# Modulations moved to VectorE, memory keys moved into the norms, and the last product in token order, in a fused two-block model

## The chip, the cores and the metric

The kernel runs as one launch on one core of a Trainium2 chip. The metric is the device time of one launch in microseconds (us). The engines of the core work side by side, each with its own queue of instructions in a fixed order: TensorE (PE) multiplies matrices, VectorE (DVE), ScalarE (ACT) and GpSimd (POOL) compute element by element, SyncE (SP) issues the DMA transfers. An instruction starts when it is at the head of its queue and the semaphores that it waits for have been raised.

## The reference

Two blocks are computed one after the other for 256 tokens of width 1024, each with two layers, all in float32.

```python
for l in range(2):                                   # block 1
    mod = silu(c) @ w_ada[l] + b_ada[l]              # 1024 x 6144
    sh1, sc1, g1, sh2, sc2, g2 = split(mod, 6)
    h = rmsnorm(x, norm_mix_g[l]) * (1 + sc1) + sh1
    o = four_attention_mixers(h @ w_in[l])
    x = x + g1 * (o @ w_out[l])
    h = rmsnorm(x, norm_mlp_g[l]) * (1 + sc2) + sh2
    x = x + g2 * (square(relu(h @ w_up[l])) @ w_down[l])
x = rmsnorm(x, final_norm_g)
for l in range(2):                                   # block 2
    proj = x @ w_in_2[l]
    mem_kv = mem @ w_mem_kv_2[l]                     # keys and values of 256 memory tokens
    merged = gates . (ssd(proj), diff_attention(proj), cross_attention(proj, mem_kv))
    x = layernorm(sqrt(2) * x + merged @ w_out_2[l])
```

## The kernel before, in words

All weights come as pieces of 128x1024 floats (512 KB). `stream` lists the pieces in the order in which they are wanted, and `next_w` hands out the next one. When it does so, it also issues the DMAs of the first 8 pieces of the list and splits the first 4 of them. A piece is loaded by SyncE into one of 8 buffers `w` (L290), cast by ScalarE to a rounded high half `wh` (L300), and VectorE subtracts this from it for a low half `wl` (L302). There are 4 buffers of each half. The `w` buffer is free after the subtraction; the halves are free when PE has used them. PE multiplies by both halves: `gemm` makes 24 matmuls of a piece, in the order wh x high, wh x low, wl x high part of the activations, and all of its matmuls carry the line of `mm` (L328).

The pieces of `w_ada` are not split. A modulation (one of six column blocks of `mod`, for each of two layers) has 8 pieces, used in four steps of two. Nine of the twelve are multiplied on PE by `ada_step` (64 narrow matmuls into a bank called ada); three are computed on GpSimd by `ada_pool` in the MLPs, as a scaled sum of the pieces row by row (`rows`), of which `ada_rows` then sums the 128 partitions by four matmuls with ones. `ada_end` transposes the result and adds the bias.

Work that PE can do while something else is computed stands in a queue `e.q`, as closures under a tag: `add` appends, `fill(n)` emits the next n, `need(tag)` emits all up to the last one of a tag. So the order in which the program is written decides what stands between two steps of a chain. On each engine a scheduler may bring instructions marked by `high_priority` forward; `issue_after(i)` keeps an instruction behind instruction i.

The MLP of block 1 runs over 16 groups g: w_up of group g (two pieces into a bank g), then w_down of group g-1 (two pieces into four banks acc). The eviction of bank g is relu and square on ScalarE (L1005, L1008) and two operations on VectorE (L1009, L1010). The norms of block 1 are `rms_wide`: squares on ScalarE, folds on VectorE, a sum over partitions on PE (`st`), variance on VectorE (`rv`), the power -1/2 on GpSimd (`rsy`), a broadcast on PE (`bc`), and then `norm_apply` or, in the last norm, a split into xh and xl. In block 2 the first products of a layer are written to banks dt and g. The memory's keys (4 groups of two pieces) and values (2 groups of four) of layer 0 are computed at the start and in the last norm of block 1, those of layer 1 in the layernorm between the layers of block 2 (`mem_gemm`).

Of the kernel before, what the change touches and what calls it, by code (L numbers as in the profile page):

```python
# [16 lines left out]
P = 128  # L17
# [198 lines left out]
NW, NS = 8, 4  # L216
AHEAD_W, AHEAD_S = 8, 4
SPLIT_FIRST, NORM_FIRST = 100, 200
NU = 11
# [6 lines left out]
class Emit:  # L226
# [64 lines left out]

    def _split(self, ent):
        nc = self.nc
        key, _, w, _ = ent
        if key[0].startswith(("w_ada", "cmp_")):
            ent[3] = w
            return
# [29 lines left out]
    def mm(self, o, l, r, start, stop):  # L327
        self.nc.tensor.matmul(o, l, r, start=start, stop=stop)  # L328
# [37 lines left out]
    def tok_mm(self, ps, t, act, k, w, j, st, sp):  # L366

        wh, wl = (x[:, j * 512 : (j + 1) * 512] for x in w)
# [116 lines left out]
def block1(e, ctx, mem0):  # L485
# [3 lines left out]
    mhl, mk0, mv0 = mem0  # L489
# [13 lines left out]
    mlp_keys = lambda l: {1 + 6 * i + n: [("w_ada", *p, n)] for i, p in enumerate(ad_mlp(l)) for n in range(4)}  # L503
    MEM = 5
    a0 = ada(0, 0) + ada(0, 1)
    start = [[], a0[0:2], a0[2:4], a0[4:6], a0[6:8]]
    for k in range(MEM):
        e.stream(MEM_KEYS(0)[k], *start[k])
    for l in range(DEPTH):
# [11 lines left out]
        e.stream(("w_down", l, 15), *([("w_in1", l + 1, zorder[0])] if l + 1 < DEPTH else []), *ad_next(l))  # L521
    e.stream(*MEM_KEYS(0)[MEM:])

# [12 lines left out]
    boxes = {}  # L536
# [24 lines left out]
    def ada_pool(l, s, n):  # L561
# [1146 lines left out]
```

## Time and profile before

| | us |
|---|---|
| runs | 1838.72, 1840.98, 1836.07 |
| median | 1838.72 |
| profiled execution | 1837.75 |
| its span, first to last instruction | 1835.9 |
| PE busy in the span | 1785.1 (97%) |
| VectorE busy | 1332.7 (73%) |
| ScalarE busy | 1017.0 (55%) |
| GpSimd busy | 360.6 (20%) |

The mean granted clock of PE in the span is 0.990. The busy times of different engines lie beside each other, so they don't add up to the span.

### The profile page before, as it was taken

How to read it: one execution, taken by the hardware profiler on the slowest of the kernel's cores; microseconds unless marked ns; L12 is line 12 of the kernel's file. 1: busy time of each engine (PE TensorE's matmuls, PEld its weight loads, DVE VectorE, ACT ScalarE, POOL GpSimd, SP SyncE). 2: the span in 40 equal slices, each digit the busy share in tenths (PEclk: the TensorE clock that was granted, in tenths of full speed). 3: DMA queues.
4: the chain of work that ended last, by engine and by line, in shares of the span. 5: the costliest groups of instructions: out<-in, count | busy, mean ns of one | idle time of the engine just before them, and what ended most of it. 6: DMA issues, size and time to landing. Idle time of an engine off the chain costs nothing.

```text
span 1835.9 us, 36208 instructions
## 1 busy us (share of the span) xinstructions
PE 1785.1 (97%) x14320; PEld 1671.4 (91%) x14320; DVE 1332.7 (73%) x2204; ACT 1017.0 (55%) x1882; POOL 360.6 (20%) x291
## 2 busy tenths in 40 slices
PE   7999899999998999999999999999999999999997
PEld 6778799987878999998999999999998999999996
DVE  3566775756768655798897997566788797997565
ACT  4444444444554444567777575454556777575452
POOL 0000282800007300002444202200001444202200
PEclk9999999999998999999999999999999999999999
DMA  8874876768347655553444644465554445644451
GB/s 330 305 233 159 316 259 199 254 201 294 128 143 280 225 181 184 170 170 122 159 162 152 195 159 145 167 206 174 196 175 138 150 154 158 194 162 162 151 183 57
DMA packets 98219, 346.82 MB, mean 189 GB/s; under 512 B 12288, under 2 KB 13440, under 8 KB 97792
## 3 DMA queue, kind: packets, MB, share of 16 engines
q1 hardware_dynamic: 98048, 344.50, 55.7%
q8 instruction: 112, 1.84, 0.4%
q14 instruction: 59, 0.48, 0.1%
HBM read 339.01 MB, written 1.05 MB: 185 GB/s over the span
## 4 chain that ended last, share of the span: by engine, by line
PE 91%; DVE 3%; ACT 3%; DMA 2%; issue 1%; POOL 0%; SPq 0%; POOLq 0%; DVEq 0%; ACTq 0%
PE g L328 68%; PE acc L328 10%; PE yps L328 2%; PE ada L328 1%; PE o L328 1%; DVE wl L302 1%; PE sc L328 1%; PE ds L328 1%; ACT wh L300 1%; PE do L328 1%; PE xs L328 1%; PE xo L328 1%; ACT sb L666 1%; DMA w<-w_up 1%; PE tp L691 1%
## 5 line engine op out<-in xcount | busy, mean ns | idle before, releaser
L302 DVE TENSOR_TENSOR wl<-w,wh 128x1024 fp32r<-128x1024 f32 x518 | 664.5, 1286 | 345.5 <-ACT wh L300 342.4
L300 ACT CAST wh<-w 128x1024 fp32r<-128x1024 f32 x518 | 540.7, 1047 | 504.6 <-PE g L328 339.5
L328 PE MATMUL g<-xh,wh 128*128 128x256 f32 x1664 | 477.7, 287 | 2.1 <-ACT dv L1291 1.9
L328 PE MATMUL g<-xl,wh 128*128 128x256 f32 x1664 | 472.1, 284 | 0.0
L328 PE MATMUL g<-xh,wl 128*128 128x256 f32 x1664 | 471.5, 283 | 0.0
L328 PEld LDWEIGHTS g<-xh,wh 128*128 128x128 f32 x1664 | 319.2, 192 | 14.5 <-issue 6.2
L328 PEld LDWEIGHTS g<-xl,wh 128*128 128x128 f32 x1664 | 319.5, 192 | 0.9 <-issue 0.7
L328 PEld LDWEIGHTS g<-xh,wl 128*128 128x128 f32 x1664 | 319.6, 192 | 0.0
L328 PE MATMUL g<-ah,wh 128*128 128x256 f32 x736 | 212.1, 290 | 6.8 <-ACT ah L591 6.7
L328 PE MATMUL g<-ah,wl 128*128 128x256 f32 x736 | 211.6, 288 | 1.2 <-DVE wl L302 1.2
L328 PE MATMUL g<-al,wh 128*128 128x256 f32 x736 | 211.5, 288 | 0.7 <-DVE al L592 0.5
L394 POOL TENSOR_TENSOR rsy<-rv,mhalf 128x2 f32<-128x2 f32 (+1 forms) x14 | 15.2, 1088 | 937.6 <-DVE rv L411 828.4
L328 PE MATMUL acc<-pt,wh 128*128 128x256 f32 x1024 | 182.9, 280 | 0.0
L1485 POOL PARTITION_BROADCAST E<-rows x64 | 95.2, 1547 | 387.9 <-PE tw L1192 185.4
L328 PEld LDWEIGHTS acc<-pt,wh 128*128 128x128 f32 x1024 | 156.8, 188 | 0.5 <-issue 0.4
L1484 ACT ACTIVATE E<-E,ltok 128x128 f32<-128x128 f32 x384 | 124.4, 394 | 59.2 <-POOL E L1485 55.5
L328 PEld LDWEIGHTS g<-ah,wh 128*128 128x128 f32 x736 | 143.0, 195 | 11.0 <-ACT ah L591 7.6
L328 PEld LDWEIGHTS g<-al,wh 128*128 128x128 f32 x736 | 143.5, 195 | 2.8 <-DVE al L592 2.0
L328 PEld LDWEIGHTS g<-ah,wl 128*128 128x128 f32 x736 | 143.4, 195 | 2.3 <-DVE wl L302 1.6
L328 PE MATMUL acc<-pt,wl 128*128 128x256 f32 x512 | 142.3, 279 | 0.0
L570 POOL TENSOR_SCALAR sb<-w,ca 128x1024 f32<-128x1024 f32 x24 | 90.0, 3750 | 61.9 <-PE ada L328 32.8
L328 PEld LDWEIGHTS acc<-pt,wl 128*128 128x128 f32 x512 | 96.2, 188 | 0.0
(384 smaller groups left out, 3386.3 us busy)
## 6 DMA issues: line engine op xcount, KB each, us to landing
w<-w_ada SPq DMA_DIRECT2D x96, 512.0 KB
w<-w_up SPq DMA_DIRECT2D x64, 512.0 KB
w<-w_down SPq DMA_DIRECT2D x64, 512.0 KB
w<-w_br SPq DMA_DIRECT2D x64, 512.0 KB
w<-w_gl SPq DMA_DIRECT2D x48, 512.0 KB
w<-w_in SPq DMA_DIRECT2D x36, 512.0 KB
w<-w_xs SPq DMA_DIRECT2D x32, 512.0 KB
w<-w_z SPq DMA_DIRECT2D x32, 512.0 KB
```

Of the source, the lines that this page charges most:

```text
L300: nc.scalar.copy(wh, w)
L302: nc.vector.tensor_tensor(wl, w, wh.bitcast(F32), ALU.subtract)
L328: self.nc.tensor.matmul(o, l, r, start=start, stop=stop)
L394: self.nc.gpsimd.tensor_tensor(y, v, self.mhalf[:, 0:cols], ALU.pow)
L570: nc.gpsimd.tensor_scalar(dst, w, ca[:, 2 * n + i : 2 * n + i + 1], None, ALU.mult)
L666: nc.scalar.activation(self.src(i), self.src(i), AF.Exp, bias=nmx[:, i : i + 1], scale=scale, accum_out=den[:, i : i + 1])
L691: nc.tensor.transpose(tp[:, h * P : (h + 1) * P], src(h), e.ident)
L1484: ex = lambda o, s, r: nc.scalar.activation(o, o, AF.Exp, bias=bias[:, s, r : r + 1])
L1485: nc.gpsimd.partition_broadcast(E, state["rows"][32 * (h % 4) : 32 * (h % 4) + 1, :])
```

## The change

- `ada_vec` takes the place of `ada_pool`: the scaled sum of a modulation's pieces runs on VectorE, one multiply-add of 128x1024 for each piece. `issue_after(last["ev"].ins)` puts each behind the latest eviction of an MLP bank. Six modulations go this way, five of them in layer 0's MLP and one in layer 1's; PE keeps six.
- `next_w` splits up to 4 pieces that need it and loads up to 6 others ahead, unsplit ones or `w_ada`; the `w` buffers go from 8 to 6.
- The keys of layer 1's memory are computed in block 1, in the norms (`filler`, `mem_fill`); `rms_wide` emits a given number of fillers before the statistics, between them and the broadcast, and behind it. Only the values stay in block 2's layernorm. Layer 0's last value group fills the last norm as before.
- At the start, half of a memory group stands behind the last modulation.
- The last product finishes the first 128 tokens, then the others in two halves of 256 columns.

```diff
-NW, NS = 8, 4
-AHEAD_W, AHEAD_S = 8, 4
+NW, NS = 6, 4
...
     def next_w(self, *key):
-        for i, ent in enumerate(self.wq[:AHEAD_W]):
-            self._fetch(ent)
-            if i < AHEAD_S and ent[3] is None:
-                self._split(ent)
+        split = raw = 0
+        for ent in self.wq:
+            if not self._whole(ent) and split < NS:
+                split += 1
+                self._fetch(ent)
+                if ent[3] is None:
+                    self._split(ent)
+            elif raw < NW:
+                raw += 1
+                self._fetch(ent)
+                if self._whole(ent):
+                    ent[3] = ent[2]
+            else:
+                break
...
-    def rms_wide(self, pool, x, eps):
+    def rms_wide(self, pool, x, eps, before=0, between=0, behind=0):
         box = []
+        self.fill(before)
         with self.tc.high_priority(offset=NORM_FIRST):
             for j in range(4):
                 self.square(pool, box, flat(x[:, 2 * j : 2 * j + 2, :]))
-            return self.rstd(pool, self.fold_sum(box), D, eps)
+            st = self.fold_sum(box)
+        with self.tc.issue_after(self.last_mm.ins):
+            self.fill(between)
+        with self.tc.high_priority(offset=NORM_FIRST):
+            bc = self.rstd(pool, st, D, eps)
+        with self.tc.issue_after(self.last_mm.ins):
+            self.fill(behind)
+        return bc
...
-    ad_early = lambda l: ada(l, 2) if l == 0 else []
+    ad_early = lambda l: ada(0, 2) if l == 0 else ada(1, 4)
-    ad_norm = lambda l: ada(l,5) if l == 0 else ada(l,4)
-    ad_mlp = lambda l: [(1,0),(1,1)] if l == 0 else [(1,5)]
-    ad_next = lambda l: ada(l+1,2)+ada(l+1,3)
+    ad_mlp = lambda l: [k for p in ([(0, 5)] + [(1, s) for s in range(4)] if l == 0 else [(1, 5)]) for k in ada(*p)]
+    def mlp_keys(l):
+        out = {}
+        for j, key in enumerate(ad_mlp(l)):
+            out.setdefault(1 + (3 * j // 4 if l == 0 else 2 * j), []).append(key)
+        return out
+    mem1 = MEM_KEYS(1)
+    filler = [mem1[0:1], mem1[3:4], mem1[1:3], MEM_KEYS(0)[MEM:]]
...
-        e.stream(("w_out1", l, 2), ("w_out1", l, 3), ("w_up", l, 0), *ad_norm(l))
+        e.stream(("w_out1", l, 2), ("w_out1", l, 3), ("w_up", l, 0), *filler[l], ("w_up", l, 1))
         nxt = mlp_keys(l)
         for g in range(16):
+            e.stream(*nxt.get(g, []))
+            if g > 1:
+                e.stream(("w_up", l, g))
             if g >= 1:
-                e.stream(("w_up", l, g))
                 e.stream(("w_down", l, g - 1))
-            e.stream(*nxt.get(g, []))
...
-    def ada_pool(l, s, n):
+    def ada_vec(l, s, n):
         if n == 0:
-            boxes[l, s] = e.t(ap_, [P, 1536], "sb", bufs=2)[:, 0:D]
+            i = boxes["n"] = boxes.get("n", -1) + 1
+            if i % 2 == 0:
+                boxes["rows"] = e.unit("rows")
+            boxes[l, s] = boxes["rows"][:, i % 2 * D : (i % 2 + 1) * D]
         rows = boxes[l, s]
         for i in range(2):
-            nc.gpsimd.tensor_scalar(dst, w, ca[:, 2 * n + i : 2 * n + i + 1], None, ALU.mult)
-            if not first:
-                nc.gpsimd.tensor_tensor(rows, rows, dst, ALU.add)
+            w, c = e.next_w("w_ada", l, s, n), ca[:, 2 * n + i : 2 * n + i + 1]
+            with tc.issue_after(last["ev"].ins):
+                if n == 0 and i == 0:
+                    nc.vector.tensor_scalar(rows, w, c, None, ALU.mult)
+                else:
+                    nc.vector.scalar_tensor_tensor(rows, w, c, rows, ALU.mult, ALU.add)
+        if n == 3:
+            e.q.insert(min(6, len(e.q)), ("mlp", lambda: ada_rows(l, s)))
...
         if l:
-            bc0 = norm_stats(x)
+            bc0 = norm_stats(x, 2, 1, 1)
             e.need("next")
...
-        ada_add("norm", ad_norm(l))
-        bc0 = norm_stats(x)
+        mem_fill("norm", filler[l])
+        bc0 = norm_stats(x, 1, 1)
...
-        ada_add("next", ad_next(l))
+        mem_fill("next", filler[DEPTH + l])
...
-        for t in range(2):
-            ps = e.gbank("g")
-            for k in range(KC):
-                e.tok_mm(ps, t, hl, k, ws[k // 2], k % 2, k == 0, k == KC - 1)
-            ev(ps, 1, t)
-            norm(t)
+        for t, cols in ((0, (0, 512)), (1, (0, S)), (1, (S, 512))):
+            ps = e.gbank("g")[:, cols[0] : cols[1]]
+            with tc.issue_after(e.last_mm.ins):
+                for k in range(KC):
+                    e.tok_mm(ps, t, hl, k, ws[k // 2], k % 2, k == 0, k == KC - 1, cols)
+            ev(ps, 512 + cols[0], t)
+            if cols[1] == 512:
+                norm(t)
...
-        for i in range(6):
+        for i in range(4, 6):
             mem_gemm(e, l + 1, i, mhl, nmk, nmv)
```

How the instructions lie now is seen at three places. The first is VectorE's queue in layer 0's MLP before the change: L302 makes a low half wl of a piece w, L1009 and L1010 evict a bank g of w_up.

```order
L302 TENSOR_TENSOR wl_2569<-w_2471,wh_2567 128x1024
L302 TENSOR_TENSOR wl_2579<-w_2503,wh_2577 128x1024
L302 TENSOR_TENSOR wl_2667<-w_2571,wh_2665 128x1024
L302 TENSOR_TENSOR wl_2697<-w_2581,wh_2695 128x1024
L1009 TENSOR_TENSOR pt_461_2633<-pt_461_2633,g_2576 128x512
L1010 TENSOR_TENSOR pt_462_2635<-pt_461_2633,pt_462_2635 128x512
L302 TENSOR_TENSOR wl_2706<-w_2607,wh_2704 128x1024
```

An eviction stands behind four splits. After the change VectorE's queue in the same MLP reads as follows; L1054 and L1055 are the eviction, L604 is the new multiply-add on a piece of `w_ada` (w_2596, w_2599), L301 the split. w_2765 and w_2801 are the two w_up pieces of group 4, w_2831 and w_2861 those of w_down in group 3, g_2738 the bank of w_up in group 3.

```order
L1054 TENSOR_TENSOR pt_483_2795<-pt_483_2795,g_2738 128x512
L1055 TENSOR_TENSOR pt_484_2797<-pt_483_2795,pt_484_2797 128x512
L604 SCALAR_TENSOR_TENSOR rows_2588<-w_2596,ca_99,rows_2588 128x1024
L604 SCALAR_TENSOR_TENSOR rows_2588<-w_2599,ca_99,rows_2588 128x1024
L301 TENSOR_TENSOR wl_2769<-w_2765,wh_2767 128x1024
L301 TENSOR_TENSOR wl_2805<-w_2801,wh_2803 128x1024
L301 TENSOR_TENSOR wl_2835<-w_2831,wh_2833 128x1024
L301 TENSOR_TENSOR wl_2865<-w_2861,wh_2863 128x1024
L1054 TENSOR_TENSOR pt_500_2928<-pt_500_2928,g_2871 128x512
L1055 TENSOR_TENSOR pt_501_2930<-pt_500_2928,pt_501_2930 128x512
```

Two modulation pieces now stand between the eviction of group 3's bank and the splits for group 4. The DMAs of these pieces in SyncE's queue after the change:

```order
L289 DMA w_2596<-w_ada 128x1024
L289 DMA w_2599<-w_ada 128x1024
L289 DMA w_2602<-w_up 128x1024
L289 DMA w_2606<-w_up 128x1024
L289 DMA w_2636<-w_down 128x1024
L289 DMA w_2672<-w_down 128x1024
L289 DMA w_2702<-w_ada 128x1024
L289 DMA w_2732<-w_ada 128x1024
L289 DMA w_2735<-w_ada 128x1024
L289 DMA w_2739<-w_ada 128x1024
L289 DMA w_2765<-w_up 128x1024
L289 DMA w_2801<-w_up 128x1024
```

The load of w_2765 stands behind those of four further modulation pieces. In the built program it waits for VectorE's L604 on w_2596, whose buffer it takes, and the load of w_2801 for that on w_2599; the load of w_2702 waits for the multiply-add ahead of these.

The third place is PE's queue in the layernorm between the layers of block 2, where st is the sum for the variance, bc the broadcast, and g_ banks with mh and ml are memory products. Before the change the broadcast stands among memory products:

```order
L328 MATMUL g_15232<-wl_15090,mh_14644 128x512
L328 MATMUL g_15232<-wh_15088,ml_14645 128x512
L328 MATMUL g_15239<-wh_15088,mh_14644 128x512
L328 MATMUL bc_15127<-pack_1_70,rsy_15125 128x128 x2
L328 MATMUL g_15239<-wl_15090,mh_14644 128x512
```

After the change the last memory product, the statistics, the broadcast and the first product of the next layer (dt, from xh) follow one another:

```order
L337 MATMUL g_15181<-wl_15170,mh_14803 128x512
L337 MATMUL g_15181<-wh_15168,ml_14804 128x512
L337 MATMUL st_15207<-ones_72,fold_15120 128x1 x2
L337 MATMUL bc_15214<-pack_1_70,rsy_15212 128x128 x2
L337 MATMUL dt_15293<-xh_15255,wh_15188 128x256
L337 MATMUL g_15332<-xh_15255,wh_15217 128x256
L337 MATMUL g_15394<-xh_15255,wh_15294 128x256
L337 MATMUL dt_15293<-xl_15256,wh_15188 128x256
L337 MATMUL dt_15293<-xh_15255,wl_15190 128x256
```

The memory products that stood behind the broadcast are gone from here.

## Rows read from the trace of the kernel before

**Rows 1.** The page's part 1, share of the span of each engine.

```profile
PE 1785.1 (97%) x14320; PEld 1671.4 (91%) x14320; DVE 1332.7 (73%) x2204; ACT 1017.0 (55%) x1882; POOL 360.6 (20%) x291
```

**Rows 2.** Windows: the MLP of layer 0 (window, length, busy us (instructions) by engine, granted clock, DMA).

```profile
232.00:396.00 164.00, 164.00 (x1386) 162.91 (x1385) 108.19 (x89) 76.23 (x87) 82.60 (x26) 1.00 0.69 228
```

**Rows 3.** Chain of waits in two groups of that MLP (start, length, what).

```profile
268.87 5.76 PE g L328 x48
274.63 5.66 PE acc L328 x48
```

**Rows 4.** Timeline of DVE in the same groups (start, length, operation, idle before and its releaser).

```profile
272.75 1.23 DVE L302 TENSOR_TENSOR wl<-w,wh 128x1024 fp32r<-128x1024 f32 x1 [1.65 <-ACT wh L300]
...
276.79 0.69 DVE L1009 TENSOR_TENSOR pt<-pt,g 128x512 f32<-128x512 f32 x1
277.52 0.69 DVE L1010 TENSOR_TENSOR pt<-pt,pt 128x512 fp32r<-128x512 f32 x1
```

**Rows 5.** Timeline of ACT in the same groups.

```profile
271.67 1.05 ACT L300 CAST wh<-w 128x1024 fp32r<-128x1024 f32 x1 [1.83 <-PE g L328]
...
275.50 0.59 ACT L1005 ACTIVATE pt<-g 128x512 f32<-128x512 f32 x1
```

**Rows 6.** Timeline of SyncE's DMA issues, before the MLP and within it.

```profile
205.43 1.87 SPq L290 DMA_DIRECT2D w<-w_up  x2
...
258.01 0.80 SPq L290 DMA_DIRECT2D w<-w_up  x2
```

**Rows 7.** Timeline of PE where it waits (start, norm and last norm of block 1, attention).

```profile
62.31 0.50 PE L328 MATMUL g<-ah,wh 128*128 128x256 f32 x2 [2.53 <-ACT ah L591]
...
204.72 3.66 PE L328 MATMUL ada<-w,ca 128*32 128x256 f32 x64
...
210.02 0.71 PE L328 MATMUL bc<-pack,rsy 128*128 128x128 f32 x4 [1.10 <-POOL rsy L394]
...
408.18 0.64 PE L328 MATMUL ada<-w,ca 128*32 128x256 f32 x8 [1.36 <-DMA w<-w_ada]
...
481.68 1.08 PE L328 MATMUL o<-pt,z 128*64 128x256 f32 x4 [2.13 <-ACT pt L693]
...
554.00 1.22 PE L328 MATMUL bc<-pack,rsy 128*128 128x128 f32 x4 [4.49 <-POOL rsy L394]
...
757.53 0.71 PE L328 MATMUL bc<-pack,rsy 128*128 128x128 f32 x4 [1.05 <-POOL rsy L394]
...
759.36 0.38 PE L328 MATMUL dt<-xh,wh 128*128 128x256 f32 x1 [1.12 <-ACT xh L455]
```

**Rows 8.** Windows behind four of these waits (PEclk is the granted clock).

```profile
213.70:220.50 6.80, 6.21 (x27) 5.92 (x28) 6.24 (x15) 3.13 (x8) 3.36 (x2) 0.50 1.03 418
...
481.00:484.50 3.50, 2.82 (x23) 1.92 (x24) 3.42 (x16) 1.37 (x4) 0.00 (x0) 1.00 0.05 19
...
551.60:561.80 10.20, 6.29 (x28) 6.18 (x29) 7.06 (x16) 2.91 (x7) 7.22 (x3) 0.50 1.01 408
...
759.80:763.20 3.40, 3.40 (x18) 3.38 (x17) 3.40 (x10) 1.72 (x5) 0.00 (x0) 0.50 0.43 147
```

**Rows 9.** Groups by form: DVE's multiply-add of 128x1024 (count, busy us, mean ns).

```profile
L1221 DVE SCALAR_TENSOR_TENSOR r<-r,mv,gb 128x1024 f32<-128x1024 f32 x2 | 2.6, 1276 | 0.0
```

**Rows 10.** Timeline of ACT ahead of that MLP.

```profile
209.14 1.04 ACT L300 CAST wh<-w 128x1024 fp32r<-128x1024 f32 x1 [2.71 <-DMA w<-w_up]
```

**Rows 11.** Timeline of DVE in the second block's layernorm.

```profile
1292.19 0.16 DVE L411 TENSOR_SCALAR rv<-st 128x2 f32<-128x2 f32 x1 [1.39 <-PE st L328]
...
1296.92 0.86 DVE L1671 SCALAR_TENSOR_TENSOR lt<-r,pack,bc 128x256 f32<-128x256 f32 x2
```

**Rows 12.** Timeline of GpSimd (POOL) there.

```profile
1292.44 0.73 POOL L394 TENSOR_TENSOR rsy<-rv,mhalf 128x2 f32<-128x2 f32 x1 [126.06 <-DVE rv L411]
```

**Rows 13.** Chain of waits at the end of the span.

```profile
1825.83 0.69 DVE r L1212
...
1829.85 0.17 DVE rv L1219
...
1831.63 0.75 DVE r L1224
```

More of the change, by code (lines that the diff above doesn't have):

```diff
@@ L327, in mm @@
     def mm(self, o, l, r, start, stop):
-        self.nc.tensor.matmul(o, l, r, start=start, stop=stop)
+        self.last_mm = self.nc.tensor.matmul(o, l, r, start=start, stop=stop)
     def gemm(self, tag, keys, act, evac, tok=False, half=None):
@@ L488, in block1 @@
     cp, zp, ap_ = pool("c1"), pool("z1"), pool("a1")
-    mhl, mk0, mv0 = mem0
+    mhl, mk0, mv0, mk1 = mem0
     cT = e.p0["cT"]
@@ L495, in block1 @@
     zorder = (0, 1, 2, 3, 5, 4, 6, 7, 8)
-    ad_early = lambda l: ada(l, 2) if l == 0 else []
+    ad_early = lambda l: ada(0, 2) if l == 0 else ada(1, 4)
     ad_mix = lambda l: ada(l, 3) + ada(l, 4) if l == 0 else []
-    ad_norm = lambda l: ada(l,5) if l == 0 else ada(l,4)
-    ad_mlp = lambda l: [(1,0),(1,1)] if l == 0 else [(1,5)]
-    ad_next = lambda l: ada(l+1,2)+ada(l+1,3)
-    mlp_keys = lambda l: {1 + 6 * i + n: [("w_ada", *p, n)] for i, p in enumerate(ad_mlp(l)) for n in range(4)}
+    ad_mlp = lambda l: [k for p in ([(0, 5)] + [(1, s) for s in range(4)] if l == 0 else [(1, 5)]) for k in ada(*p)]
[4 more added lines that the diff above has]
+        return out
     MEM = 5
+    mem1 = MEM_KEYS(1)
+    filler = [mem1[0:1], mem1[3:4], mem1[1:3], MEM_KEYS(0)[MEM:]]
     a0 = ada(0, 0) + ada(0, 1)
-    start = [[], a0[0:2], a0[2:4], a0[4:6], a0[6:8]]
+    start = [[], a0[0:2], a0[2:4], a0[4:6], []]
     for k in range(MEM):
         e.stream(MEM_KEYS(0)[k], *start[k])
+    half = e.wq[-2:]
+    del e.wq[-2:]
+    e.stream(*a0[6:8])
+    e.wq.extend(half)
     for l in range(DEPTH):
@@ L534, in block1 @@
     mods = [e.t(cp, [P, 48], f"mod{l}") for l in range(DEPTH)]
-    boxes = {}
+    boxes, last = {}, {}
     def ada_step(l, s, n):
@@ L580, in ada_add, with norm_stats @@
         for key in keys:
-            e.add(tag, lambda key=key: (ada_pool if tag == "mlp" else ada_step)(*key[1:]))
-    def norm_stats(src):
-        return e.rms_wide(ap_, src, 1e-6)
+            e.add(tag, lambda key=key: (ada_vec if tag == "mlp" else ada_step)(*key[1:]))
+    def norm_stats(src, *filler):
+        return e.rms_wide(ap_, src, 1e-6, *filler)
     def norm_apply(src, bc, A, sh, ah, al):
@@ L597, in block1 @@
         ada_add(f"start{g}", start[g])
+    half = e.q[-2:]
+    del e.q[-2:]
+    ada_add("start4", a0[6:8])
+    e.q.extend(("start5", fn) for _, fn in half)
     b_ada = e.p0["b_ada"]
@@ L706, in out, with mem_fill @@
                     e.split(oh[:, base + c, :], ol[:, base + c, :], o[c][:, :S])
+    hl = []
+    def mem_fill(tag, steps):
+        for key in steps:
+            mem_gemm(e, key[1], MEM_KEYS(key[1]).index(key), hl[-1], *((mk0, mv0) if key[1] == 0 else (mk1, None)), tag)
     def mixers(l, ah, al, oh, ol, ev_x):
@@ L967, in mixers @@
         e.need("I")
+        hl.append(load_mem(e))
         e.need("ad")
@@ L1043, in down_last @@
                     part(c, (m, m + 1))
-        def late_mem():
-            with tc.issue_after(last["dve"].ins), tc.issue_after(last["act"].ins):
-                box.append(load_mem(e))
-        parts, box, last = {}, [], {}
+        parts = {}
         steps = mlp_keys(l)
         for g in range(17):
-            if l + 1 == DEPTH and g == 1:
-                e.add("mlp", late_mem)
             if g < 16:
@@ L1061, in block1 @@
             ada_add("mlp", steps.get(g, []))
-            for i, p in enumerate(ad_mlp(l)):
-                if g == 6 * i + 8:
-                    e.add("mlp", lambda p=p: ada_rows(*p))
         e.need("mlp")
-        ada_add("next", ad_next(l))
+        mem_fill("next", filler[DEPTH + l])
         for k in range(KC):
             nc.vector.scalar_tensor_tensor(x[:, k, :], acc[k // 2][:, (k % 2) * S : (k % 2 + 1) * S], mod[:, 40 + k : 41 + k], x[:, k, :], ALU.mult, ALU.add)
-    for k in range(MEM, 6):
-        mem_gemm(e, 0, k, box[0], mk0, mv0)
-    bc = norm_stats(x)
-    e.need("mem")
+    bc = norm_stats(x, 2, 1, 1)
+    e.need("next")
     xh, xl = v3(e.unit("xh", F32R), KC), v3(e.unit("xl", F32R), KC)
@@ L1081, in block1, with block2 @@
     return xh, xl
-def block2(e, ctx, xh, xl, mk, mv, out):
+def block2(e, ctx, xh, xl, mk, mv, mk1, out):
     nc, tc, d = e.nc, e.tc, e.d
@@ L1207, in finish, with ev @@
                 nc.scalar.activation(r[:, t, q * 512 : (q + 1) * 512], ps, AF.Copy, scale=ALPHA)
-        stats = e.t(tp_, [P, 2, 2, 6], "stats")
-        def ev(ps, g, t):
-            rg = r[:, t, g * 512 : (g + 1) * 512]
+        stats = e.t(tp_, [P, 2, 4, 6], "stats")
+        def ev(ps, c0, t):
+            rg = r[:, t, c0 : c0 + ps.shape[1]]
             nc.vector.tensor_tensor(rg, ps, rg, ALU.add)
-            nc.vector.bn_stats(out=stats[:, t, g, :], in_=rg)
+            for i in range(0, ps.shape[1], S):
+                nc.vector.bn_stats(out=stats[:, t, (c0 + i) // S, :], in_=rg[:, i : i + S])
         def norm(t):
```

31 lines of the change are left out of this document (13 added, 18 removed).

## The prediction, made before the changed kernel was run

> **What bounds the kernel now.** The page's table of engines comes first: TensorE (PE) is busy for 97% of the span [rows 1], so the time is PE's work plus the few microseconds in which PE waits or runs at half clock. Each edit is therefore priced by what it does to PE. Next the table by windows: in the MLP of layer 0 (232 to 396 us, the stretch into which the change puts most of its new work) PE is busy for 164.00 of 164 us at a granted clock of 1.00, and VectorE (DVE) for 108.19 [rows 2]. There is nothing to gain for PE there, only something to lose, while DVE has 56 us left. The chain of waits shows the pattern: two products of w_up (g, 5.76 us) and two of w_down (acc, 5.66 us), a group every 11.42 us, with no wait between them [rows 3].
>
> The timelines of DVE, ScalarE (ACT) and of SyncE's DMA issues in one group show why. The low half wl of a piece of weights takes 1.23 us on DVE, the two steps of an eviction 0.69 us each [rows 4]; the cast to wh takes 1.05 us on ACT and the eviction's first step 0.59 [rows 5]. Two w_up pieces are issued at 258.01 [rows 6], and the first is cast only at 271.67 [rows 5], when a buffer of halves comes free: weights land some 10 us before they are wanted. That distance is the cover that the change touches.
>
> PE's timeline around the norms shows where it does wait now: 2.53 us at the start, 1.10 in the first norm, 1.36 ahead of layer 1, 4.49 in layer 1's norm, 1.05 and 1.12 in the last norm; in the first MLP norm the 64 products of a modulation take 3.66 us [rows 7]. Behind such waits PE runs for a while at a granted clock of 0.50, the 1.2 GHz level: for 6.80, 10.20 and 3.40 us [rows 8]; half of that is lost. The shortest such stretch, 3.4 us, costs 1.7 us. The wait of 2.13 us at 481.68 [rows 7] was followed by a clock of 1.00 [rows 8], so not every wait is.
>
> **The change part by part.** Durations are those of the profiled execution: 1837.75 us, 1835.9 of it span, about 1 us below the median of the runs (1838.72).
>
> *The wait it adds.* Five modulations, 40 pieces, now go through DVE in layer 0's MLP, each operation placed behind the latest eviction, and the `w` buffers, shared by these pieces and w_up and w_down, go from 8 to 6. The order shows the consequence: the buffer into which w_up's w_2765 is loaded is the one that the modulation piece w_2596 leaves. DVE reads w_2596 only behind the eviction of bank g_2738, the bank of the w_up product before. So the load of the next group's weights, issued groups ahead before, cannot start until that product is done. From the product's end, in series: ACT 0.59 and DVE 0.69 + 0.69 [rows 4, 5], 2.0 us, say 2.1 with the hand-overs; the modulation's operation on 128x1024, which the MLP does not contain now: its nearest row is the same operation on the same shape in the last layernorm, 1.28 us [rows 9]; the load: on an idle queue two w_up pieces issued at 205.43 [rows 6] let ACT cast at 209.14, as soon as the first landed [rows 10], 3.7 us; the cast 1.05; wl 1.23, on which the third matmul waits. Together 9.4, and 9.6 with hand-overs between five engines. Meanwhile PE has the two w_down pieces before it, already split: 5.66 us, and two matmuls that need wh alone, 0.24. That leaves 3.6 us of waiting. Behind the waiting load the next three pieces queue on SyncE, but each follows its predecessor at about the pace at which PE uses them, so I count no more for them.
>
> How often: the 20 steps of two pieces lie on groups 1 to 15, four on every three groups, and in the built order the load of a group's first w_up piece takes a modulation's buffer in nine of the sixteen groups: once near the start (2.8 us, as there its cover is longer by the last matmuls of the norm's fill, an estimate), four times in the form above (3.6), and four times behind four modulation operations in a row, where the first frees the buffer, the other three lie beside the load, and a few small matmuls of the modulation's end give 0.3 us more cover (3.3). Sum 2.8 + 14.4 + 13.2 = 30.4 us. Bounds: an eviction in before, held up by a cast and a wl of the next group, ended at 278.21, 3.6 us after its product ended at 274.63 [rows 3, 4], 1.5 more than the 2.1 used, so at most 44; with everything 1 us faster per event, 21. I stay near the sum of rows, because the casts that delayed that eviction are just those that now come late.
>
> The Trainium skill (DMA: Bandwidth & Descriptors, section "Anatomy of one DMA") gives 2.0 us plus bytes over 436 GB/s for one transfer, fitted on the GpSimd path, so 3.2 us for these 512 KB where this trace shows 3.7 from issue to cast. By the page the nine waits would be 4.5 us shorter together and the forecast about 1857.
>
> *The clock behind these waits.* Waits of 3.3 to 3.6 us lie between the one of 2.13 us without and that of 4.49 with a half-clock stretch [rows 7, 8]. I take seven in ten: 9 x 0.7 x 1.7 = 10.7 us; between 0 and 15.
>
> *Modulations off PE.* Nine of twelve stand on PE now, six afterwards; each removed saves 3.66 us [rows 7] and costs four matmuls over the finished rows, 0.6 us at most by the pace of the 64. 3 x 3.06 = -9.2 us. The DVE work, 40 x 1.28 = 51 us in layer 0 and 10 in layer 1, fits the 56 us that DVE has idle there as busy time; if DVE were full, it would come on top. Layer 1's eight pieces are spread out, no w_up load waits just behind one, so I add no stall there. The GpSimd work that goes hid completely.
>
> *Memory groups in the norms.* In layer 1's norm the 4.49 us came from DVE and ACT queues held by a load; this load moves away and about 3 us go (0 to -4). In the first norm PE waits 1.10 and then for the split, and memory-key work takes the place of the modulation that covered it: 0 (-2 to +3). Ahead of layer 1 the modulation loads that PE waits for go: -1. In the last norm a piece goes between the chain's steps and covers the two waits and a part of the half-clock stretch: -2.5.
>
> *The gap it opens.* In the second block's layernorm, memory work covers PE today; half of it moves away. By the order, the last memory product now stands ahead of the second statistics, and nothing between these, the broadcast and the first dt product. The chain there is rv 0.16 [rows 11], rsy 0.73 [rows 12], broadcast, two lt of 0.43 each [rows 11], xh: about 3 us, with some clock +4 (3 to 7; 0 if the fill ends later than the folds).
>
> *Start.* The last half of a memory group behind the last modulation covers the 2.53 us and its half-clock stretch: -3.5 (0 to -5).
>
> *Last product.* Token half 0 is finished before half 1, so only half 1's chain is left after the last matmul. Today 1825.83 to 1831.63 passes from the last bank's addition to the last scaling [rows 13], with half 0's operations between; half of that, about -2.5 (0 to -3.5), after 0.3 more for narrower matmuls.
>
> *Prefetch rule.* Up to four pieces split and six raw ones instead of eight in all: where no modulations stand it reaches deeper, and PE did not wait for weights: 0 +/- 3.
>
> Sum without the MLP: -9.2 - 3 - 1 - 2.5 + 4 - 3.5 - 2.5 = -17.7. With the waits +30.4 and the clock +10.7: +23.4, thus 1837.75 + 23.4 = 1861 us.
>
> **The rivals.** (a) *The waits, but short*: a load returns faster and no half-clock stretch follows. Two and a half us each, 22 in all, net +5: 1843. For it: PE's queue has small fillers; against it: each term is a row. (b) *The cover holds (faster)*: the load of w_2765 starts before the eviction, or reaches SBUF while PE still has work, as 10 us ahead today. Then the rest is left: 1820. It turns at 17.7 / 9 = 2.0 us of waiting per event without a clock loss: below, the change is a gain. Against it: DVE runs its queue in order, and the operation stands behind the eviction. (c) *The waits add up*: the eviction stays 3.6 us late, the load shares the queue with four modulation pieces, and every wait brings a half-clock stretch: 44 + 15 - 17.7 = +41, 1879.
>
> **How the numbers follow.** Main case (1848 to 1874) 0.60; (a) 0.18; (b) 0.12; (c) 0.10. Beyond 0.3% (5.5 us, about what a measurement of this kernel can tell from no change) slower are the main case, (c), and half of (a); the other half of (a) is the same. Slower 0.79, same 0.09, faster 0.12. The range, 1836 to 1879, leaves out (b) and the ends of (a) and (c).
>
> **What would show it.** After: in the layer 0 MLP nine waits of PE of 3 to 4 us ahead of a w_up product, ended by wl or wh and behind them a load, with stretches at clock 0.50; the stretch some 40 us longer; DVE busy above 140 us in it. Fewer modulation matmuls (384 instead of 576); no wait of 4.49 us in layer 1's norm; PE's wait near 3 us before the first dt of the second block's second layer. I am wrong if w_up is cast without waiting for its load in that stretch: then (b).

## The result, and the profile after

| | us |
|---|---|
| changed kernel, runs | 1900.28 to 1905.40, median 1902.22 |
| kernel before, runs beside it | 1836.07 to 1840.98, median 1839.53 |
| ratio, 95% interval | 1.0345 [1.0323, 1.0368] |
| span of the profiled execution | 1898.8 (before 1835.9) |

The change makes the kernel 62.7 us slower. The forecast was 1861 us, slower, for a wait in layer 0's MLP; the sign and the place were right, the size was not.

The page of the changed kernel, part 1 and the granted clock in 40 slices of the span (compare [rows 1]):

```profile
PE 1809.2 (95%) x14176; PEld 1691.7 (89%) x14176; DVE 1354.4 (71%) x2259; ACT 1019.2 (54%) x1884; POOL 211.0 (11%) x246
...
PEclk9999988889899899999999999999999999999999
```

PE is busy for 95% in place of 97% of a span 63 us longer, and the clock row shows a run of 8s, the sixth to the ninth slice, in the MLP of layer 0. The window of this MLP, from the first product into acc to the last (columns as in [rows 2]):

```profile
239.30:470.90 231.60, 196.99 (x1490) 190.03 (x1488) 141.22 (x138) 81.09 (x95) 0.00 (x0) 0.90 0.68 224
```

Before, the same stretch took 173.91 us, all of it busy, at a clock of 1.00:

```profile
229.05:402.96 173.91, 173.91 (x1466) 172.27 (x1464) 115.27 (x101) 80.56 (x93) 85.46 (x27) 1.00 0.68 226
```

It now takes 231.60, of which PE is busy for 196.99. So 34.6 us are waits, and the busy time itself grew by 23.1 us, at a granted clock of 0.90. VectorE is busy for only 141 of 232 us: it isn't full.

The chain of waits in one group (start, length, what; compare [rows 3]):

```profile
257.22 5.66 PE acc L337 x48
262.88 5.78 PE g L337 x48
...
268.68 0.61 ACT pt L1050
...
269.31 0.64 ACT pt L1053
...
269.97 0.70 DVE pt L1054
...
270.73 0.57 issue
271.31 1.29 DVE rows L604
...
272.61 3.80 DMA w<-w_up
...
276.49 1.05 ACT wh L299
...
277.59 0.50 PE g L337 x2
278.09 0.77 PE ada L337 x8
```

This is the chain of the prediction, step by step. The product of w_up ends at 268.66; then come the two ACT steps and the two DVE steps of its eviction, the multiply-add on a modulation's piece (rows, L604, 1.29 us), the load of the next w_up piece (3.80), its cast (1.05), and at 277.59 the next product. In the meantime PE had only the 5.66 us of the w_down products, listed here in the group before. PE's timeline has such a wait nine times, as often as forecast. In five of the nine the operation ahead of the load is the scaled first piece of a modulation (L602, 0.75 us) and not a multiply-add. Five of the waits are:

```profile
247.84 0.58 PE L337 MATMUL g<-ah,wh 128*128 128x256 f32 x1 [2.62 <-ACT wh L299]
...
277.59 0.39 PE L337 MATMUL g<-ah,wh 128*128 128x256 f32 x1 [3.29 <-ACT wh L299]
...
372.92 0.58 PE L337 MATMUL g<-ah,wh 128*128 128x256 f32 x1 [5.24 <-ACT wh L299]
...
389.58 0.39 PE L337 MATMUL g<-ah,wh 128*128 128x256 f32 x1 [1.90 <-ACT wh L299]
...
420.64 0.58 PE L337 MATMUL g<-ah,wh 128*128 128x256 f32 x1 [5.46 <-ACT wh L299]
```

The nine waits are 2.62, 3.29, 2.67, 3.45, 3.22, 5.24, 1.90, 5.46 and 3.57 us, 31.4 together; the rest of the 34.6 are waits of under 1 us for wl. Windows over stretches at these five waits show the clock (the number before the last two of a row):

```profile
247.60:254.40 6.80, 6.09 (x27) 5.80 (x28) 4.29 (x4) 3.32 (x4) 0.00 (x0) 0.50 0.84 311
278.30:281.70 3.40, 3.40 (x21) 2.85 (x14) 1.72 (x2) 1.04 (x1) 0.00 (x0) 0.50 0.46 152
370.50:377.30 6.80, 4.38 (x22) 3.35 (x23) 2.45 (x2) 2.09 (x2) 0.00 (x0) 0.50 0.39 134
391.00:394.40 3.40, 3.40 (x17) 3.40 (x18) 1.23 (x1) 1.38 (x2) 0.00 (x0) 0.50 0.86 287
418.30:425.10 6.80, 4.46 (x22) 3.43 (x23) 2.45 (x2) 2.09 (x2) 0.00 (x0) 0.50 0.45 140
```

Each of the nine waits has such a stretch at 0.50. The four of 3.4 us begin up to 1.4 us after the wait's end, the five of 6.8 us 0.2 to 2.4 us before it, so part of the latter lies in the wait itself. They last 47.6 us in all. PE is busy for 39.90 us of them; half of this, 20.0 us, is an estimate of what the clock cost.

Where the whole time went, by stages whose ends are first or last instructions in PE's timeline (us; single profiled executions, so a stage can differ by 2 or 3 us without a cause in the code). The work moved is PE time of memory pieces (2.88 us each) and modulations (3.66) that changed their stage:

```
stage, up to                         before   changed  difference  work moved  rest
first product with w_in                62.3     64.6      +2.3        0.0       +2.3
last product with w_out, layer 0      142.2    147.3      +5.1        0.0       +5.1
first product into acc (norm)          24.5     27.4      +2.9       +2.1       +0.8
last product into acc (MLP)           173.9    231.6     +57.7       +2.6      +55.1
last product with w_out, layer 1      142.2    157.0     +14.9       +7.9       +7.0
first product into acc (norm)          27.1     28.6      +1.5       +2.1       -0.6
last product into acc (MLP)           173.2    172.3      -1.0        0.0       -1.0
first dt product (last norm)           14.0     16.3      +2.3        0.0       +2.3
last matmul (block 2)                1066.1   1046.0     -20.1      -23.0       +3.0
end of the span                        10.5      7.8      -2.7        0.0       -2.7
```

The 2.6 us of work in the MLP are taken from the last experiment below, where the same MLP ran without a wait. What PE waits for elsewhere in the changed kernel (compare [rows 7]):

```profile
64.61 0.58 PE L337 MATMUL g<-ah,wh 128*128 128x256 f32 x1 [3.63 <-ACT ah L625]
...
218.48 0.58 PE L337 MATMUL st<-ones,fold 128*128 128x1 f32 x4 [3.43 <-DVE fold L444]
...
836.92 0.60 PE L337 MATMUL st<-ones,fold 128*128 128x1 f32 x4 [2.88 <-DVE fold L444]
...
1377.97 0.71 PE L337 MATMUL bc<-pack,rsy 128*128 128x128 f32 x4 [1.06 <-POOL rsy L403]
1379.90 0.39 PE L337 MATMUL dt<-xh,wh 128*128 128x256 f32 x1 [1.22 <-ACT xh L1709]
```

At the start the wait of 2.53 us has become 3.63. In layer 0's norm and in the last norm PE now stands at the statistics, for 3.43 and 2.88 us, since the folds on VectorE are not ready; in layer 1's norm it does so at 634.50, for 3.43 us too. The last two rows are the chain laid bare in block 2's layernorm: 1.06 and 1.22 us, for the forecast 3 to 4. The end of the chain of waits (compare [rows 13]):

```profile
1891.31 0.43 DVE r L1246
...
1892.23 0.28 DVE mv L1253
...
1892.53 0.17 DVE rv L1254
...
1894.31 0.75 DVE r L1259
```

From the last bank's addition to the last scaling 3.0 us pass, where it was 5.8.

### The profile page after: what moved, and what is told of

It reads as the page before. It is cut to its first block, busy times and chain, and to the rows that moved or that the text cites. A ratio compares the mean times of both kernels' runs of the same rounds, so it can differ in the third digit from the quotient of the medians.

```text
span 1898.8 us, 35935 instructions
## 1 busy us (share of the span) xinstructions
PE 1809.2 (95%) x14176; PEld 1691.7 (89%) x14176; DVE 1354.4 (71%) x2259; ACT 1019.2 (54%) x1884; POOL 211.0 (11%) x246
## 3 DMA queue, kind: packets, MB, share of 16 engines
HBM read 340.06 MB, written 1.05 MB: 180 GB/s over the span
## 4 chain that ended last, share of the span: by engine, by line
PE 82%; DMA 6%; DVE 6%; ACT 3%; issue 2%; POOL 0%; SPq 0%; POOLq 0%; DVEq 0%; ACTq 0%
PE g L337 64%; PE acc L337 7%; DVE wl L301 2%; DMA w<-w_up 2%; ACT wh L299 2%; PE yps L337 1%; DMA w<-w_in 1%; PE o L337 1%; PE ada L337 1%; PE ds L337 1%; PE sc L337 1%; DMA w<-w_out 1%; DMA w<-w_mv 1%; PE do L337 1%; PE uq L337 1%
## 5 line engine op out<-in xcount | busy, mean ns | idle before, releaser
L301 DVE TENSOR_TENSOR wl<-w,wh 128x1024 fp32r<-128x1024 f32 x518 | 640.3, 1238 | 360.4 <-ACT wh L299 353.0
L337 PE MATMUL g<-ah,wh 128*128 128x256 f32 x736 | 218.3, 299 | 37.9 <-ACT wh L299 31.4
L337 PE MATMUL g<-ah,wl 128*128 128x256 f32 x736 | 218.6, 298 | 3.2 <-DVE wl L301 3.2
L337 PE MATMUL g<-al,wh 128*128 128x256 f32 x736 | 216.9, 296 | 1.3 <-DVE al L626 1.3
L337 PEld LDWEIGHTS g<-ah,wh 128*128 128x128 f32 x736 | 149.9, 205 | 42.1 <-ACT wh L299 34.1
L337 PEld LDWEIGHTS g<-ah,wl 128*128 128x128 f32 x736 | 150.3, 205 | 8.2 <-DVE wl L301 7.5
L337 PEld LDWEIGHTS g<-al,wh 128*128 128x128 f32 x736 | 150.4, 205 | 2.0 <-DVE al L626 1.9
L1303 DVE SCALAR_TENSOR_TENSOR cv<-g,pack,cv 128x254 f32<-128x254 f32 (+1 forms) x192 | 89.1, 475 | 2.5 <-ACT cv L1300 0.7
```

The source lines that it names most:

```text
L301: nc.vector.tensor_tensor(wl, w, wh.bitcast(F32), ALU.subtract)
L337: self.last_mm = self.nc.tensor.matmul(o, l, r, start=start, stop=stop)
L1303: nc.vector.scalar_tensor_tensor(a_[:, a:b], p_[:, a + j - 2 : b + j - 2], conv_w[:, i0 + j : i0 + j + 1], a_[:, a:b], ALU.mult, ALU.add)
```

## Experiments

Theory 1: the load of w_up waits for a buffer that a multiply-add, queued behind an eviction, holds; that and the clock behind it make the MLP's loss. Rivals: VectorE is too full; the DMA queue is. Theory 5: the losses outside the MLP come from the `w` buffers, 6 for 8. Times are compared with runs of the kernel before on the same chip, and versions of the changed kernel by their distance from these; the changed kernel's is 62.7 us. The change also raises the number of large units (`NU`) from 11 to 12, which its description leaves out.

**Eight buffers.**

```diff
-NW, NS = 6, 4
+NW, NS = 8, 4
-NU = 12
+NU = 11
```

> The changed kernel with 8 buffers w in place of 6 (and 11 large units in place of 12, to make the room); up to 8 unsplit pieces may be loaded ahead. The multiply-adds stay behind the evictions. Theory 1 (the load of w_up waits for a buffer that a multiply-add behind an eviction holds): in the built order the load of a group's first w_up piece now takes a buffer freed by a split ahead of the eviction, so the nine waits go; layer 0's MLP falls from 231.6 us to 174 to 180, the whole to 1840 or so. Rival 2 (VectorE's queue is too full: 40 multiply-adds of 1.3 us delay the splits whatever the buffers): the MLP stays above 215. Rival 3 (the loads are slow as the queue carries more bytes there): the MLP stays above 205, and loads take longer than 4 us.

1867.97 us, ratio to before 1.0171 [1.0151, 1.0191]: 29.7 us above the kernel before, so 33 of the 62.7 are gone. The MLP's window:

```profile
236.50:427.70 191.20, 181.72 (x1486) 176.71 (x1486) 138.29 (x142) 80.62 (x94) 0.00 (x0) 0.98 0.82 273
```

It falls from 231.6 to 191.2 us, not to 174 to 180: the nine waits of 1.9 to 5.5 us are gone, but others are left, 9.5 us together, the longest 2.3. That one in the chain of waits:

```profile
296.05 2.28 DVE wl L301 x2
...
298.35 6.78 DMA w<-w_up
...
305.20 1.05 ACT wh L299
```

The load now waits for a split in VectorE's queue, which stands behind a multiply-add, and takes 6.78 us, with the DMA engines busy for 82% of the window. So theory 1 holds for most of the loss. That a fuller DMA queue makes up the rest is not shown: the last experiment below moves more bytes per second in this MLP, 300 GB/s against 273, without any wait. Block 2 takes 1054.8 us up to the last matmul, 8.9 more than in the changed kernel. This may be the price of the unit taken away, but buffers and units were changed together, and the kernel before has 11 units too.

**Multiply-adds not tied to an eviction**, 6 buffers.

```diff
-            with tc.issue_after(last["ev"].ins):
+            if True:
                 if n == 0 and i == 0:
```

> The changed kernel with the multiply-adds of layer 0's and layer 1's MLP not held behind the latest eviction; 6 buffers as in the changed kernel. Theory 1: the scheduler places them ahead of the eviction, the buffers come free earlier, the nine waits go though the buffers stay 6; layer 0's MLP 174 to 185 us, the whole 1840 to 1850. Rival 2 (VectorE too full): waits stay, MLP above 215. Rival 4 (6 buffers alone are too few with pieces in this order): about half of the waits stay, MLP near 200.

1870.58 us, 1.0176 [1.0158, 1.0193], 32.3 above the kernel before. The windows of the norm and of the MLP:

```profile
210.40:249.60 39.20, 26.85 (x181) 24.84 (x180) 28.83 (x42) 14.70 (x23) 0.70 (x1) 0.91 0.62 198
249.60:432.70 183.10, 176.00 (x1465) 171.29 (x1464) 126.11 (x131) 78.00 (x91) 0.00 (x0) 1.00 0.77 263
```

The MLP falls to 183.1 us at a clock of 1.00, with 6 buffers: so these alone don't make the nine waits. But the norm ahead of it grew from 27.4 to 39.2 us: the scheduler now puts multiply-adds between the steps of norm_apply on VectorE (24 matmuls of w_up, 2.9 us, also moved across the border of the two stages). Layer 1's norm grew likewise, from 28.6 to 34.5 us, 2.9 of it moved work. So the MLP came out as expected and the whole did not.

**Behind the eviction before the latest.** One line of the changed kernel in effect:

```diff
-                last["ev"] = nc.vector.tensor_tensor(ul, r, uh.bitcast(F32), ALU.subtract)
+                last["prev"], last["ev"] = last.get("ev"), nc.vector.tensor_tensor(ul, r, uh.bitcast(F32), ALU.subtract)
...
-            with tc.issue_after(last["ev"].ins):
+            with tc.issue_after((last["prev"] or last["ev"]).ins):
```

> The changed kernel with each multiply-add of the MLPs held behind the eviction before the latest one, nothing else changed; 6 buffers. In the built order the load of a group's first w_up piece then takes a buffer freed ahead of the eviction of the group before. Theory 1: the nine waits go, layer 0's MLP 175 to 195 us and the norm ahead of it unchanged (27.4), since the multiply-adds cannot move into the norm as they did with no such tie; the whole 1845 to 1860. If full queues (VectorE or DMA) are the cause: above 205, the whole above 1872.

1853.87 us, 1.0099 [1.0082, 1.0116], 17.0 above the kernel before, so 46 of the 62.7 are gone. The MLP's window:

```profile
237.10:423.00 185.90, 178.79 (x1492) 174.32 (x1490) 139.74 (x142) 81.18 (x95) 0.00 (x0) 1.00 0.83 286
```

185.9 us with the norm at 27.4 as before this edit, VectorE as busy as in the changed kernel (139.74 us against 141.22) and more bytes per second (286 GB/s against 224). Same work, same buffers, same engines; only the place in VectorE's queue differs. Both rivals fall as the main cause.

**Buffers and prefetch rule in the kernel before.** Three kernels: the changed rule with 6 buffers, the changed rule with 8, and the old rule with 6, each otherwise the kernel before. The edit of the third (the changed rule is the `next_w` of the change):

```diff
-NW, NS = 8, 4
-AHEAD_W, AHEAD_S = 8, 4
+NW, NS = 6, 4
+AHEAD_W, AHEAD_S = 6, 4
```

> The kernel before with 6 buffers and the changed prefetch rule, and nothing else of the change. Theory 5 (the losses of the changed kernel outside layer 0's MLP, +2.3 at the start, +5.1 and about +7 in the two layers' mixers, come from fewer buffers): start +2, mixers +4 to +7 each, the whole 1850 to 1856; the MLP may lose too where GpSimd's sums hold buffers. Rival 6 (they come from the new order of pieces and of work): stages within 1 us of before, the whole 1838 to 1841.

> The kernel before with the changed prefetch rule (up to 4 pieces split, up to 8 others loaded) and its 8 buffers. Theory 5a (the losses in the mixers come from the number of buffers, 6): within 2 us of before in both mixers, the whole 1837 to 1841. Theory 5b (they come from the rule: it loads further ahead and so lets urgent loads queue behind others): mixers +4 to +7 us each as with 6 buffers, the whole 1848 to 1855.

> The kernel before with 6 buffers and its own rule (first 6 pieces loaded, first 4 split). Theory 5a: mixers +4 to +7 us each, start +1 to +2, the whole 1848 to 1855. Theory 5b: within 2 us of before, the whole 1837 to 1842.

| kernel before with | us | ratio |
|---|---|---|
| changed rule, 6 buffers | 1851.65 | 1.0067 [1.0053, 1.0081] |
| changed rule, 8 buffers | 1841.55 | 1.0024 [1.0013, 1.0035] |
| old rule, 6 buffers | 1851.21 | 1.0076 [1.0058, 1.0095] |

Six buffers cost 13 to 14 us, whatever the rule; the rule alone some 4 to 5 with 8 buffers, more than the 2 that 5a allowed. By stages, 6 buffers with the old rule: start +1.3, mixers of layer 0 +5.3, MLP +2.7, then +6.7 up to layer 1's w_out: about what the changed kernel loses at the start and in the mixers. The window of layer 0's mixers, first in the kernel before:

```profile
62.30:204.50 142.20, 139.83 (x1201) 117.02 (x1202) 93.03 (x279) 63.63 (x156) 2.31 (x2) 0.99 0.68 241
```

and with 6 buffers:

```profile
63.60:211.20 147.60, 143.71 (x1202) 120.85 (x1202) 94.30 (x281) 65.11 (x157) 1.40 (x2) 0.97 0.63 232
```

PE's waits grow from 2.4 to 3.9 us, and its busy time by 3.9, with the clock at 0.97 for 0.99. ScalarE's and PE's timelines with 6 buffers show the largest of these waits and what stands ahead of it:

```profile
127.22 1.05 ACT L300 CAST wh<-w 128x1024 fp32r<-128x1024 f32 x1 [4.07 <-DMA w<-w_out]
...
131.54 0.72 PE L691 MATMUL tp<-pack,sb 128*128 128x128 f32 x3 [1.94 <-DVE sb L678]
```

ScalarE stands for 4.07 us at the cast of a piece of w_out that has not landed, and VectorE for 4.79 us at the subtraction that follows it (L302, at 128.31). Steps of the attention stand behind both in their queues, and PE then waits 1.94 us for their result (sb). With 6 buffers and the changed rule PE waits 2.53 us at this place, in the changed kernel 2.33; in the kernel before and in all five other kernels with 8 buffers it does not. Two versions of the changed kernel with 6 buffers, those with fillers placed otherwise (below), wait 0.3 us there or not at all, so the buffers alone don't decide it.

The window of layer 1's mixers, first in the kernel before:

```profile
402.90:545.10 142.20, 135.54 (x1142) 114.15 (x1142) 98.10 (x284) 67.47 (x160) 3.06 (x3) 0.99 0.55 193
```

and with 6 buffers and the old rule:

```profile
413.80:562.60 148.80, 142.07 (x1143) 118.31 (x1141) 98.08 (x284) 67.73 (x160) 3.07 (x3) 0.94 0.51 182
```

PE waits for 6.7 us in both; what is added is busy time, at a clock of 0.94 for 0.99. About half of that can be chance: in the kernel before with only its last product changed, below, the same stretch took 145.2 us for 142.1, at 0.96. In the changed kernel PE waits there for weights directly:

```profile
510.94 0.58 PE L337 MATMUL g<-wh,ah 128*128 128x256 f32 x1 [2.69 <-ACT wh L299]
```

The window of a stretch that begins just before the end of this wait:

```profile
510.40:524.10 13.70, 13.16 (x31) 6.53 (x32) 3.61 (x4) 2.69 (x4) 0.00 (x0) 0.50 0.48 167
```

All five versions of the changed kernel with 6 buffers have this wait, of 2.7 to 3.1 us; the two with 8 do not.

**Fillers placed otherwise in the norms** of the changed kernel.

```diff
-        bc0 = norm_stats(x, 1, 1)
+        bc0 = norm_stats(x, 2, 0)
...
-    bc = norm_stats(x, 2, 1, 1)
+    bc = norm_stats(x, 3, 1, 0)
```

> The changed kernel with the fillers of the norms placed otherwise: in the norms ahead of the MLPs both memory pieces ahead of the statistics (not one ahead, one between), in the last norm three ahead and one between (not two, one, one). Theory 7 (in the changed kernel the statistics wait 3 us because too little PE work stands ahead of them): the wait for the folds falls by about 2.9 us in each of the three norms; in the last norm nothing else is left open, so it falls from 16.3 to 13.4 us; in the two others the chain behind the statistics is bare again, and 1 to 3 us of it come back. Rival: the place of the fillers doesn't matter, since the sum of waits in a chain stays the same: within 1 us in all three. Whole 1893 to 1901.

1891.55 us, 1.0299 [1.0284, 1.0314], 54.6 above the kernel before, so 8 of the 62.7 are gone. The last norm, in PE's timeline:

```profile
827.44 0.61 PE L337 MATMUL st<-ones,fold 128*128 128x1 f32 x4 [0.16 <-DVE fold L444]
...
832.82 0.38 PE L337 MATMUL dt<-xh,wh 128*128 128x256 f32 x1 [1.48 <-ACT xh L473]
```

The wait at the statistics falls from 2.88 to 0.16 us, and 1.48 come back at the first dt product; the stage falls from 16.3 to 13.6 us. Layer 1's norm falls from 28.6 to 25.3, layer 0's from 27.4 to 26.0. In these two norms the wait at the statistics falls from 3.43 to 0.55 us, and 2.05 come back at the broadcast. The three stages give 7.4 us. The place of a filler counts, not only its amount.

**Parts alone in the kernel before**: the last product in token order; then also half a memory group behind the last modulation at the start. The edits are those of the change.

> The kernel before with the last product in token order and nothing else. My term was -2.5 us; the changed kernel's time from the last matmul to the end of the span fell by 2.7. Expected 1836 to 1837 against 1838.7, that is -1.5 to -3; if the half products of 256 columns cost what they save, no difference.

> The kernel before (8 buffers) with two parts of the change: the last product in token order, and half of the memory group behind the last modulation at the start. My start term was -3.5; in the changed kernel the start came out at +2.3, and with 8 buffers at -1.7. Theory (the start edit works, and 6 buffers ate it): first product of the layer 1.5 to 3.5 us earlier than before, the whole 1830 to 1834. Rival (it does nothing by itself): 1835 to 1836, as with the last product alone.

The first: 1835.37 us, 0.9984 [0.9975, 0.9992]; the second: 1835.70, 0.9988 [0.9976, 1.0000]. The last product is worth 2.9 us (1.5 to 4.6 by the interval), and the kernel with it alone is faster than the kernel before and the changed one. The start edit adds nothing that can be measured: the first product with w_in starts at 60.76 us against 61.23 without it, in single executions.

**All mends together**: both mends of queue and fillers, with 6 buffers; then with 8 buffers, 11 units and `raw < NW - NS` as the limit of unsplit pieces.

> The changed kernel with both mends: multiply-adds behind the eviction before the latest, and the fillers ahead of the statistics. If the parts add up: 1853.9 minus 8 (2.7 in the last norm, 3.3 in layer 1's norm, 1.4 in layer 0's, some more from the clock), 1844 to 1848; still slower than before, since 6 buffers cost 13 to 14 us. If the waits only move: 1850 to 1855.

> As the former with 8 buffers, 11 large units and at most 4 unsplit pieces ahead. If the buffers are what is left: start, and mixers of both layers, each some 3 to 5 us shorter than with 6 buffers, layer 0's MLP near 178; but block 2 pays 11 us for the missing unit, as in the first run with 8 buffers; the whole 1838 to 1846. If the mixers do not shorten, their loss comes from the order of the pieces: 1850 or more.

1849.96 us, 1.0075 [1.0053, 1.0097], and 1847.10, 1.0044 [1.0028, 1.0059]. The first lies between the two cases expected: the three norms gave 8.2 us, as expected, but layer 0's MLP took 189.8 us in its profiled execution for 185.9. The second is 1 us above its range. The MLP's window of the second:

```profile
228.00:404.50 176.50, 176.50 (x1491) 173.77 (x1490) 137.83 (x141) 79.92 (x95) 0.00 (x0) 1.00 0.87 300
```

No wait at all, at full clock, with all five modulations on VectorE: 176.5 us. That is 2.6 us of added PE work over before, and it leaves for the changed kernel 196.99 - 176.50 = 20.5 us of busy time lost to the clock. At the start (59.9 us) and in layer 0's mixers (143.0) the loss is gone too. Layer 1's mixers did not shorten, 162.6 us against 157.0, nor did block 2, 1057.6 against 1046.0, so both versions stay slower than before. In block 2 it goes with 8 buffers and 11 units together, as in the first experiment (8.9 us there, not 11). In layer 1's mixers the wait for weights is gone, but in both versions with 8 buffers PE waits 3.8 us in seven pieces for VectorE's steps of the attention, and in this one a stretch of 17.1 us at a clock of 0.50 lies over most of them; why these steps come late was not tried out.

## Why the prediction was right in kind and wrong in size

The net was forecast as +23.4 us, with a range that ended at 1879 us; the profiled spans differ by 62.9. By its own terms:

| term | forecast | measured | read from |
|---|---|---|---|
| waits for w_up in the MLP | +30.4 | +34.6 | window, 231.60 - 196.99 |
| clock behind them | +10.7 | +20.5 | 196.99 less 176.50 of the last experiment |
| modulations off PE | -9.2 | -8.3 | sum of the work moved |
| prefetch rule and buffers, mixers | 0 | +5.1 and, with the loads ahead of layer 1 (forecast -1), +7.0 | stages less work |
| start | -3.5 | +2.3 | stage |
| norms, layers 0 and 1 | 0 and -3 | +0.8 and -0.6 | stages less work |
| last norm | -2.5 | +2.3 | stage |
| block 2's layernorm | +4 | +3.0 | stage less work |
| last product | -2.5 | -2.7 | stage |
| layer 1's MLP | 0 | -1.0 | stage |

In layer 0's MLP 41.1 us were forecast, waits and clock, and 55.1 came; rival (c) had 59 there. Outside of it the sum was forecast as -17.7 us and came out as +7.8, which is 25.5 of the 39.5 us missed.

**The added wait** was right: the mechanism, the nine places and the cover of 5.66 us. That single waits came out near the forecast 3.6 us is in part luck. The series left out the second step of the eviction on ScalarE, 0.64 us, so that 2.65 us and not 2.1 passed from the product's end to VectorE's operation; against it, in the wait shown above, the matmuls of ada that follow the first two (0.77 us) took the place of a further wait for wl, and in five of the nine the operation took 0.75 us and not 1.28. (9.6 less 5.90 us of cover is also 3.7, not 3.6.) The load took longer than the 3.7 us of the forecast: from issue to cast 3.3 to 5.8 us in the nine, 4.5 on average. Two of the nine waits were 5.2 and 5.5 us: in them the load took 5.75 and 5.54 us; that other pieces in the queue slowed it is likely, but was not shown. The test named for it was met: each of the nine casts waited for its load. The two experiments that change only the multiply-adds' place, and the one with 8 buffers, show that it is the tie of buffer, queue and eviction, and not a full engine. By the fit in the Trainium skill (DMA: Bandwidth & Descriptors, "Anatomy of one DMA"), measured on the GpSimd path, the load is estimated at 3.2 us. The shortest of the nine, issued at 385.15 and cast at 388.48, took 3.3, and two loads of w_down in the same MLP took 3.2 until they landed; the average of the nine, 4.5, lies on the other side of the 3.7 forecast, so these loads do not bear out the shorter time.

**The clock** was mis-sized by half: "I take seven in ten", times the shortest stretch of 3.4 us. It was nine in nine, and five stretches were twice as long. The discount rested on one row, a wait of 2.13 us without a stretch. [rows 7] and [rows 8] had stretches behind waits both smaller and larger: 6.8 us behind 1.10 and 2.64 (the latter at 213.76, not among the rows), 3.4 behind 1.05 and 1.12, 10.2 at 4.49. And that row does not repeat: in the kernel before with only its last product changed, the same wait, 2.14 us at 483.41, was followed by 3.4 us at 0.50:

```profile
485.00:488.40 3.40, 3.40 (x18) 2.35 (x16) 1.61 (x11) 0.74 (x2) 0.00 (x0) 0.50 0.45 154
```

**The step that failed** is first of all the prefetch term: "PE did not wait for weights: 0 +/- 3". It is the largest error outside the MLP, 12 to 13 us; the clock term in the MLP, 10 us short, is the next. The 10 us by which weights land early had been read in layer 0's MLP alone, and [rows 7] even held a wait of 1.36 us for a piece of `w_ada`. The kernel before with 6 buffers and the changed rule, and nothing else, is 13.3 us slower. In layer 0's mixers a late load of w_out holds ScalarE's queue, and PE waits 2.33 us, in the changed kernel, for the attention's steps behind it. In layer 1's mixers of the changed kernel PE waits 2.69 us for a piece of weights itself, with 13.7 us at a clock of 0.50. That these waits are the whole of +5.1 and +7.0 us is not shown: with 8 buffers layer 0's mixers took 146.1 us in the first experiment and 143.0 in the last, and layer 1's did not shorten. I had priced what 6 buffers do only where the multiply-adds stand.

**The gains in the norms and at the start** were taken as the waits that the fillers stand beside, without asking for the longest chain to the next step. Two memory pieces, 5.8 us, or one, 2.9, do not reach from the last product to the folds, so the wait moved from the broadcast to the statistics; one more piece ahead of these took all but 0.2 to 0.6 us of it away. At the start 6 buffers are part of it (+1.3 us in the kernel before), but the edit itself, in the kernel before with its 8, is worth at most some 1.5 us (62.3 to 60.8, of which 1.1 without it too), not 3.5; the two versions of the changed kernel with 8 buffers came to 60.6 and 59.9.

The signs of the rest were right: the removed work (384 modulation matmuls in place of 576, as forecast), the gap in block 2 and the last product came within 1 us. In layer 1's norm the wait of 4.49 us is gone, as forecast, but 3.43 us at the statistics took most of its place.

## What to carry to other kernels

When loads ahead of use take their buffers from one rotating pool, a prefetch is only as early as the slowest reader of the buffer that it inherits: follow each load to the instruction whose buffer it takes, and from there to what that instruction is queued behind. Moving 48 operations, 40 of them in layer 0's MLP, one eviction earlier, with nothing else changed, gave back 46 of 63 us. A filler has to reach from where the chain starts to the step at which PE next stands. A cut in buffers has to be priced in every stage that uses the pool, also where PE does not wait for the weights themselves: a cast that waits for its load holds up what stands behind it in the same queue.

## What had not been expected of the hardware

All nine waits of 1.9 to 5.5 us in the MLP, although PE had worked for 14 us and more without a wait ahead of each, came with 3.4 or 6.8 us at a granted clock of 0.50, which cost 20.5 us on top of the 34.6 of the waits. With the multiply-adds one eviction earlier, seven waits of 0.5 to 1.3 us in the same MLP left the clock at 1.00. A wait of 2.1 us at one place in the attention had no such stretch in one execution and 3.4 us in another. The scaled first piece of a modulation on VectorE (L602, no addition) took 0.75 us for 128x1024 where the multiply-add took 1.28.
